# 288 empty bytes ahead of the residual stream's tile

## The chip, the cores and the metric

The kernel runs on one core of one Trainium2 chip. The metric is the device time of one execution in microseconds (us), from three runs. The profile is of one execution; its span is the time from the first to the last instruction of the program.

## The reference

A decoder trunk of two layers on a residual stream x of 512 tokens by 1024 channels, in float32:

```
for l in range(DEPTH):                                   # DEPTH = 2
    x = x + 0.5 * swiglu_ffn(x, ffn1_norm[l], ffn1_w_gate[l], ffn1_w_up[l], ffn1_w_down[l])
    h = rms_norm(x, mix_norm[l])
    p = h @ w_in[l]                                      # columns split into four head groups
    y = concat[pool_mixer, rwkv7_mixer, nsa_mixer, short_conv_mixer]
    x = x + y @ w_out[l]
    x = x + 0.5 * swiglu_ffn(x, ffn2_norm[l], ffn2_w_gate[l], ffn2_w_up[l], ffn2_w_down[l])

def swiglu_ffn(x, g, w_gate, w_up, w_down):              # D_FF = 2816
    h = rms_norm(x, g)
    return (jax.nn.silu(h @ w_gate) * (h @ w_up)) @ w_down
```

Most of the work is in the projections: gate, up and down of two FFNs in each layer, w_in and w_out.

## The kernel before

**Layout.** Activations lie transposed: channels on the 128 partitions, the 512 tokens along the row. x is one tile of 8 x 512 float32, 16,384 bytes in each partition.

**The split projection.** Every projection runs in `mm3` (lines 209 to 211). A float32 weight tile w is cut by `split` into two fp32r tiles, wh (`cut`, line 203, ScalarE) and wl, the rest (line 204, VectorE). The activations are split in the same way: hh and hl for a normed input, ah and al for the gated FFN middle, yh and yl for the mixers' output. Each slice k of 128 input channels then takes three matmuls of a stationary 128x128 weight slice by a moving 128x512 tile, wh by hh, wh by hl, wl by hh, all added up in one PSUM tile:

```
for k in range(n):
    sl = slice(k * P, (k + 1) * P)
    self.nc.tensor.matmul(ps, wh[:, sl], xh[:, k], start=(first and k == 0), stop=False)
    self.nc.tensor.matmul(ps, wh[:, sl], xl[:, k], start=False, stop=False)
    self.nc.tensor.matmul(ps, wl[:, sl], xh[:, k], start=False, stop=(last and k == n - 1))
```

**An FFN** (`ffn`) has two halves of 11 blocks. A block has 8 slices for gate and 8 for up, so 48 matmuls into the PSUM tiles d and r, and gives one slice of ah and al. Behind each half stands a down projection: 8 output tiles with 11 slices each, so 33 matmuls for each, into d and n in turn. FFN1 reads hh and hl from the pool `hp`. FFN2 reads another pair of tiles of the same names and shapes, from the pool `h2`, which `mix` opens behind x. The output projection (w_out, in `mix`) reads yh and yl, which lie in `hp` again.

**Weights** come by DMA through two tiles w (1024 KB for gate and up of one block, 704 KB for a down tile) and through two tiles each of wh and wl.

**The mixers** (`mixers`) work between w_in and w_out, with many small matmuls. For them x is closed (`self.xes.close()`) and its place is given to the pool `mp`; x goes to DRAM (xd) before and comes back after. Inside them, L670 is the last step of the compressed keys' scores, L573 the product of attention weights and values.

**Order.** The tile framework orders each engine's instructions by a simulated timeline and places the pools one behind the other in each partition. The places that matter here, in bytes from the start of the partition's row, are these (x is opened anew by `open_x` after each set of mixers, at the same place):

| tile | pool | begins at | remainder of 512 |
|---|---|---|---|
| hh (and yh) | hp | 29,920 | 224 |
| hl (and yl) | hp | 46,304 | 224 |
| w, two | wst | 62,688 and 70,880 | 224 |
| wh, two | wsp | 79,072 and 83,168 | 224 |
| wl, two | wsp | 87,264 and 91,360 | 224 |
| small tiles | sm | 95,456 | |
| t, five of 2,080 bytes | tp | 98,592 | |
| sq | xp | 108,992 | 448 |
| x | xp | 111,040 | 448 |
| ah, al in FFN1 | ap | 127,424 and 149,952 | 448 |
| hh, hl for FFN2 | h2 | 127,424 and 143,808 | 448 |
| ah, al in FFN2 | ap | 160,192 and 182,720 | 448 |
| the mixers' tiles | mp | 108,992 up to 228,992 | various |

The slices of hh, hl, ah and al are 2,048 bytes long and those of wh and wl 512, so all slices of a tile begin at the tile's remainder.

Of the kernel before, what the change touches and what calls it, by code (L numbers as in the profile page):

```python
# [10 lines left out]
F32 = mybir.dt.float32  # L11
# [7 lines left out]
P = 128  # L19
# [79 lines left out]
class Net:  # L99
# [266 lines left out]
    def open_x(self):  # L366
        self.xes = ExitStack()
        xp = self.xes.enter_context(self.tc.tile_pool(name=self.nm("xp"), bufs=1))
        self.sq = xp.tile([P, S], F32, tag="sq", name=self.nm("sq"))
        self.x = xp.tile([P, NCH, S], F32, tag="x", name=self.nm("x"))  # L370

    def mt(self, name, shape, dt=F32, bufs=None):
# [777 lines left out]
```

## Time and profile before

| what | us |
|---|---|
| median of 3 runs | 2114.76 |
| lowest, highest run | 2101.97, 2114.92 |
| the profiled execution, first to last instruction | 2112.0 |
| TensorE busy in it | 2086.9 |
| VectorE, ScalarE, GpSimd busy | 998.0, 683.4, 258.0 |

The profiled execution's own time is its span, 2112.0; what lies around the span is not in the trace, and the median of the runs is 2.76 above it. The busy time of TensorE is the time in which at least one matmul was under way; matmuls overlap each other, so one can last longer than the distance to the next. In the names, PE is TensorE and PEld its weight load, DVE VectorE, ACT ScalarE, POOL GpSimd. `d<-hh,wh` is a matmul into the PSUM tile d of the moving tile hh by the weight tile wh; L209 is line 209 of the kernel.

### The profile page before, as it was taken

Reading aid. Unit: us, or ns where it says so; the run is one execution under the profiler, and the core shown is the slowest. Engines: PE = TensorE matmul, PEld = TensorE weight load, DVE = VectorE, ACT = ScalarE, POOL = GpSimd, SP = SyncE. Lnnn points to the kernel's source line nnn. Section 1 sums busy time; section 2 is a strip of 40 time slices with the busy share of each in tenths; the row PEclk is TensorE's granted clock in tenths of the full one; section 3 lists DMA queues with packets and bytes.
Section 4 is the critical chain, followed back from the end, with each engine's and each line's share of the span. In section 5 each row is a group of like instructions: output and inputs, shape, how many; then the busy total and the mean of one; then the engine's idle time right before and its main releaser. Section 6 shows DMA issues by size and latency. Waiting matters only on the chain.

```text
span 2112.0 us, 25358 instructions
## 1 busy us (share of the span) xinstructions
PE 2086.9 (99%) x10262; PEld 1662.1 (79%) x10262; DVE 998.0 (47%) x1792; ACT 683.4 (32%) x1101; POOL 258.0 (12%) x249
## 2 busy tenths in 40 slices
PE   8999999999999999999999999999999999999999
PEld 6888888777668888888888888887776688888887
DVE  5434434567555443433544344356674544334333
ACT  4222323332464322222332223233324643222221
POOL 1100111113001110011011001110120011100110
PEclk9999999999799999999999999999996999999999
DMA  5223224324003222322322232242240032223223
GB/s 201 89 86 107 95 88 132 110 86 116 36 2 110 98 82 83 108 100 81 109 97 87 91 103 93 92 137 84 95 119 21 1 119 81 94 83 113 94 84 91
DMA packets 60438, 195.20 MB, mean 92 GB/s; under 512 B 29344, under 2 KB 29472, under 8 KB 45600
## 3 DMA queue, kind: packets, MB, share of 16 engines
q1 hardware_dynamic: 57760, 185.18, 27.2%
q0 software_dynamic: 2560, 8.39, 1.1%
q8 instruction: 80, 1.31, 0.3%
q14 instruction: 38, 0.31, 0.0%
HBM read 183.58 MB, written 8.93 MB: 91 GB/s over the span
## 4 chain that ended last, share of the span: by engine, by line
PE 97%; DVE 2%; ACT 0%; issue 0%; DMA 0%; SPq 0%; DVEq 0%
PE d L209 15%; PE d L211 15%; PE d L210 15%; PE r L211 8%; PE r L210 8%; PE r L209 8%; PE n L210 5%; PE n L211 5%; PE n L209 5%; PE o L573 2%; PE d L544 2%; PE n L561 1%; PE r L935 1%; PE n L622 1%; PE c L826 1%; PE c L823 0%
## 5 line engine op out<-in xcount | busy, mean ns | idle before, releaser
L203 ACT CAST wh<-w 128x1024 fp32r<-128x1024 f32 (+2 forms) x360 | 343.9, 955 | 1113.8 <-issue 333.4
L204 DVE TENSOR_TENSOR wl<-w,wh 128x1024 fp32r<-128x1024 f32 (+2 forms) x360 | 400.3, 1112 | 225.7 <-ACT wh L203 218.8
L209 PE MATMUL d<-hh,wh 128*128 128x512 f32 x1008 | 399.2, 396 | 6.9 <-ACT hh L216 6.9
L210 PE MATMUL d<-hl,wh 128*128 128x512 f32 x1008 | 397.8, 395 | 2.4 <-DVE hl L217 2.4
L211 PE MATMUL d<-hh,wl 128*128 128x512 f32 x1008 | 397.1, 394 | 0.0
L210 PE MATMUL r<-hl,wh 128*128 128x512 f32 x736 | 289.1, 393 | 0.0
L211 PE MATMUL r<-hh,wl 128*128 128x512 f32 x736 | 288.8, 392 | 0.0
L209 PE MATMUL r<-hh,wh 128*128 128x512 f32 x736 | 288.7, 392 | 0.0
L270 POOL TENSOR_TENSOR al<-t,ah 128x512 fp32r<-128x512 f32 x88 | 151.9, 1726 | 1084.5 <-ACT ah L269 1084.5
L209 PEld LDWEIGHTS d<-hh,wh 128*128 128x128 f32 x1008 | 189.8, 188 | 52.3 <-ACT hh L216 6.9
L210 PEld LDWEIGHTS d<-hl,wh 128*128 128x128 f32 x1008 | 189.8, 188 | 45.9 <-DVE hl L217 4.5
L211 PEld LDWEIGHTS d<-hh,wl 128*128 128x128 f32 x1008 | 189.9, 188 | 43.6 <-issue 2.3
L264 DVE TENSOR_TENSOR t<-d,rs 128x512 f32<-128x512 f32 x88 | 60.5, 691 | 274.3 <-PE d L211 268.3
L268 DVE TENSOR_TENSOR t<-t,r 128x512 f32<-128x512 f32 x88 | 60.5, 687 | 227.8 <-PE r L211 227.6
L210 PEld LDWEIGHTS r<-hl,wh 128*128 128x128 f32 x736 | 138.2, 188 | 30.9
L209 PEld LDWEIGHTS r<-hh,wh 128*128 128x128 f32 x736 | 138.2, 188 | 30.9
L211 PEld LDWEIGHTS r<-hh,wl 128*128 128x128 f32 x736 | 138.2, 188 | 30.8
L210 PE MATMUL d<-al,wh 128*128 128x512 f32 x352 | 139.2, 396 | 0.0
L211 PE MATMUL n<-ah,wl 128*128 128x512 f32 x352 | 139.2, 396 | 0.0
L209 PE MATMUL n<-ah,wh 128*128 128x512 f32 x352 | 139.2, 396 | 0.0
L209 PE MATMUL d<-ah,wh 128*128 128x512 f32 x352 | 139.2, 395 | 0.0
L211 PE MATMUL d<-ah,wl 128*128 128x512 f32 x352 | 139.2, 395 | 0.0
(297 smaller groups left out, 2348.6 us busy)
## 6 DMA issues: line engine op xcount, KB each, us to landing
w<-in_g SPq DMA_DIRECT2D x87, 1024.0 KB, 4.9
w<-in_d SPq DMA_DIRECT2D x64, 704.0 KB, 4.1
w<-in_win SPq DMA_DIRECT2D x20, 1024.0 KB, 4.9
w<-in_wout SPq DMA_DIRECT2D x8, 1024.0 KB, 5.8
xd<-x POOLq DMA_DIRECT2D x16, 256.0 KB, 4.1
x<-xd POOLq DMA_DIRECT2D x16, 256.0 KB, 5.6
x<-in_x SPq DMA_DIRECT2D x8, 256.0 KB, 5.4
s<-in_cmpk SPq DMA_DIRECT2D x8, 256.0 KB, 3.5
```

The lines of the kernel that those rows point to most:

```text
L203: self.nc.scalar.copy(hi, w)
L204: self.nc.vector.tensor_sub(lo, w, hi.bitcast(F32))
L209: self.nc.tensor.matmul(ps, wh[:, sl], xh[:, k], start=(first and k == 0), stop=False)
L210: self.nc.tensor.matmul(ps, wh[:, sl], xl[:, k], start=False, stop=False)
L211: self.nc.tensor.matmul(ps, wl[:, sl], xh[:, k], start=False, stop=(last and k == n - 1))
L264: nc.vector.tensor_mul(t, pg, self.rs)
L268: nc.vector.tensor_mul(th, th, pu)
L270: nc.gpsimd.tensor_sub(al, th, ah.bitcast(F32))
L544: nc.tensor.matmul(pq[:, :w], Q[j][hs, i * P:(i + 1) * P], kt[hs, :w], start=True, stop=True)
L561: nc.tensor.transpose(ptr[:, b * P:(b + 1) * P], sc[:, b * P:(b + 1) * P], self.ident)
L573: nc.tensor.matmul(po["o"][64 * hp:64 * hp + 64], VT[:, b, br * 64:br * 64 + 64], pT[:, b * P:(b + 1) * P], start=False, stop=(br == 1 and ...
L622: nc.tensor.matmul(ph[0:31, 0:P], blk[:, l], w1[:, (l % 4) * P:(l % 4 + 1) * P], start=(l == 0), stop=(l == 15))
```

## The change

`open_x` takes one more tile between sq and x, of 72 float32 values, 288 bytes in each partition. Nothing writes or reads it. x, and the pools `ap` and `h2` that stand behind it, then begin 288 bytes further on: x at 111,328, ah and al of FFN1 at 127,712 and 150,240, FFN2's hh and hl at 127,712 and 144,096, its ah and al at 160,480 and 183,008. The remainder of 512 is 224 for each of them. hp, the weights, the small tiles, sq and the mixers' tiles stay where they are.

```
         self.sq = xp.tile([P, S], F32, tag="sq", name=self.nm("sq"))
+        xp.tile([P, 72], F32, tag="gap", name=self.nm("gap"))
         self.x = xp.tile([P, NCH, S], F32, tag="x", name=self.nm("x"))
```

## Rows read from the trace of the kernel before

**Rows 1.** The page, busy time of each engine, share of the span, instructions.
```profile
PE 2086.9 (99%) x10262; PEld 1662.1 (79%) x10262; DVE 998.0 (47%) x1792; ACT 683.4 (32%) x1101; POOL 258.0 (12%) x249
```

**Rows 2.** The page, the chain that ended last, by engine and by line.
```profile
PE 97%; DVE 2%; ACT 0%; issue 0%; DMA 0%; SPq 0%; DVEq 0%
PE d L209 15%; PE d L211 15%; PE d L210 15%; PE r L211 8%; PE r L210 8%; PE r L209 8%; PE n L210 5%; PE n L211 5%; PE n L209 5%; PE o L573 2%; PE d L544 2%; PE n L561 1%; PE r L935 1%; PE n L622 1%; PE c L826 1%; PE c L823 0%
```

**Rows 3.** Windows by stage; the first line names the columns.
```profile
core 0: us, PE busy (x) PEld busy (x) DVE busy (x) ACT busy (x) POOL busy (x), PEclk, DMA share, GB/s
134.50:195.50 61.00, 61.00 (x263) 49.11 (x262) 23.38 (x31) 13.00 (x17) 1.28 (x1) 1.00 0.33 106
197.50:315.00 117.50, 117.50 (x520) 97.27 (x519) 47.51 (x54) 33.26 (x42) 18.10 (x10) 1.00 0.28 93
656.50:686.50 30.00, 30.00 (x134) 24.84 (x133) 15.74 (x20) 11.52 (x17) 5.54 (x3) 1.00 0.31 105
708.50:1057.50 349.00, 349.00 (x1497) 281.05 (x1496) 146.86 (x178) 100.53 (x131) 41.66 (x25) 1.00 0.29 94
...
1360.50:1422.00 61.50, 61.50 (x265) 49.54 (x264) 30.54 (x41) 21.97 (x32) 9.13 (x11) 1.00 0.43 135
1757.50:2106.50 349.00, 349.00 (x1497) 280.96 (x1496) 138.73 (x167) 90.87 (x116) 37.66 (x22) 1.00 0.29 93
```

**Rows 4.** Timeline of TensorE in FFN1: start, duration; first and last of 28.
```profile
219.80 0.39 PE L210 MATMUL d<-hl,wh 128*128 128x512 f32 x1
...
225.92 0.39 PE L210 MATMUL r<-hl,wh 128*128 128x512 f32 x1
```

**Rows 5.** Timeline of TensorE in FFN2: start, duration; first and last of 25.
```profile
749.79 0.40 PE L209 MATMUL r<-hh,wh 128*128 128x512 f32 x1
...
755.39 0.40 PE L209 MATMUL d<-hh,wh 128*128 128x512 f32 x1
```

**Rows 6.** Timeline of TensorE from the output projection into FFN2.
```profile
685.75 0.39 PE L210 MATMUL n<-yl,wh 128*128 128x512 f32 x1
685.97 0.39 PE L211 MATMUL n<-yh,wl 128*128 128x512 f32 x1
686.20 0.39 PE L209 MATMUL n<-yh,wh 128*128 128x512 f32 x1
686.43 0.39 PE L210 MATMUL n<-yl,wh 128*128 128x512 f32 x1
686.65 0.39 PE L211 MATMUL n<-yh,wl 128*128 128x512 f32 x1
686.88 0.40 PE L209 MATMUL d<-hh,wh 128*128 128x512 f32 x1
687.11 0.40 PE L210 MATMUL d<-hl,wh 128*128 128x512 f32 x1
687.35 0.40 PE L211 MATMUL d<-hh,wl 128*128 128x512 f32 x1
```

**Rows 7.** The page, groups of instructions: busy, mean ns | idle before, releaser.
```profile
L209 PE MATMUL d<-hh,wh 128*128 128x512 f32 x1008 | 399.2, 396 | 6.9 <-ACT hh L216 6.9
L210 PE MATMUL d<-hl,wh 128*128 128x512 f32 x1008 | 397.8, 395 | 2.4 <-DVE hl L217 2.4
...
L210 PE MATMUL d<-al,wh 128*128 128x512 f32 x352 | 139.2, 396 | 0.0
```

**Rows 8.** The page, DMA issues: KB each, us from issue to landing.
```profile
w<-in_g SPq DMA_DIRECT2D x87, 1024.0 KB, 4.9
w<-in_d SPq DMA_DIRECT2D x64, 704.0 KB, 4.1
```

**Rows 9.** Windows of TensorE, compression to end of attention, each layer: PEclk third.
```profile
532.00:641.30 109.30, 106.63 (x947) 0.86 0.03 11
1576.70:1690.60 113.90, 111.22 (x948) 0.82 0.03 11
```

**Rows 10.** The chain that ended last in order of time: start, us.
```profile
531.93 1.73 PE n L670 x16
...
641.27 1.51 PE o L573 x16
...
1576.68 1.73 PE n L670 x16
...
1690.53 1.51 PE o L573 x16
```

More of the change, by code (lines that the diff above doesn't have):

```diff
@@ L369, in open_x @@
         self.sq = xp.tile([P, S], F32, tag="sq", name=self.nm("sq"))
+        xp.tile([P, 72], F32, tag="gap", name=self.nm("gap"))
         self.x = xp.tile([P, NCH, S], F32, tag="x", name=self.nm("x"))
```

## Prediction

> **What bounds the kernel now.** I read the page's busy times first: TensorE is busy for 2086.9 of 2112.0 us [rows 1], and the chain that ended last is 97% TensorE, nearly all of it three source lines, L209 to L211, the three matmuls of the split projection [rows 2]. So the end is set by how fast these matmuls follow each other. Their busy time does not tell that: a record lasts 0.39 or 0.40 us, but the next one starts before it has ended. What counts is the **pitch**, the distance from start to start, and the change can act on nothing else, as it adds no instruction.
>
> So the second reading is the pitch by stage. In a stretch without idle time, the number of records is (width + one record) / pitch, since a record that juts into the stretch is counted too. The first layer's FFN1, second half, gate and up: (117.5 + 0.39) / 520 = 0.2267 us. FFN2 of either layer: (349.0 + 0.40) / 1497 = 0.2334 us. The down projection of FFN1: (61.0 + 0.40) / 263 = 0.2335 us. The output projection: (30.0 + 0.39) / 134 = 0.2268 us [rows 3]. The timeline gives the same two numbers more finely: 27 starts from 219.80 to 225.92, so 226.7 ns, and 24 starts from 749.79 to 755.39, so 233.3 ns [rows 4, 5].
>
> Now the third reading: what do the slow stretches share? The clock is granted in full in all of them [rows 3], the tile shapes are equal, the weights come through the same two pairs of buffers. FFN1 and FFN2 run the very same code. The one thing that splits them is where the moving tile lies: hh, hl, yh and yl in the pool hp at remainder 224 are fast; ah, al and FFN2's hh, hl, all behind x at remainder 448, are slow. The switch falls on one instruction: between 685.75 and 686.65 us the output projection steps by 0.22 to 0.23 with records of 0.39, and from 686.88 on, the first matmul that reads FFN2's hh, records are 0.40 long and steps 0.23 to 0.24 [rows 6]. In rows 4 and 5 the pitch is also the same over all eight weight slices of a tile, which lie 512 bytes apart, and when the second weight buffer takes over. So if the pitch hangs on how moving and weight tile lie to each other, it repeats every 512 bytes.
>
> **The change part by part.** It is one edit with one direct effect: x and all that is stacked on it move up by 288 bytes, and 448 + 288 = 736 = 512 + 224. Behind it ah, al, and FFN2's hh and hl begin at remainder 224, as the weights and the tiles of hp do.
>
> - Matmuls that move to the fast offset. Down projections: six groups (three terms, two accumulators) of 352, of which one is shown, 2112 matmuls [rows 7]. FFN2 gate and up: 22 blocks x 2 x 8 slices x 3 = 1056 in each layer, 2112 in both. Sum 4224.
> - Gain of each: 233.3 - 226.7 = 6.67 ns [rows 4, 5]. 4224 x 6.67 = **28.2 us**. All of it lies on the path, because TensorE has no idle time in these stretches [rows 3]. I take the full 6.67 since the other end of the comparison is the same code on tiles at the very remainder that the moved ones get. The bounds for this term are 0 (the remainder is not the cause) and 28.2.
> - What is late next: the supply of weights. At the fast pitch a gate/up block takes 48 x 226.7 = 10.9 us and its 1024 KB land in 4.9; a down block takes 33 x 226.7 = 7.5 us and its 704 KB land in 4.1 [rows 8], with two buffers. FFN1 already feeds the fast pitch with the same loads. In the busiest down stretch VectorE works 30.54 of 61.5 us and ScalarE 21.97 [rows 3]; 3% less room does not matter. If that cover were gone in the down stages alone, their half of the gain, 14.1 us, would be lost.
> - What else moves: x changes its remainder for VectorE, ScalarE, GpSimd and the DMAs. No row shows what that does to such an instruction. The nearest rows are TensorE's waits on the feed that reads x, 6.9 and 2.4 us in the whole run [rows 7]; if those instructions changed by a tenth either way, it would be 1 us. I take zero and keep +-1. The tiles of the mixers do not move at all, since they are opened when x is closed; the norm's sq lies ahead of the gap. FFN2's al, the highest tile behind x, ends at byte 205,248, below the mixers' top at 228,992, so nothing is pushed out.
>
> The profiled span falls from 2112.0 to 2083.8. The median of the runs shown is 2.76 us above that span; I carry this over: 2114.76 - 28.2 = **2086.6 us**, 1.3% less. About 1%, 21 us here, is what a measurement of this kernel can tell from no change, so the forecast lies just beyond.
>
> The unchanged part has a spread that matters more than this sum's error. In the stage from the compression to the end of attention the granted clock averages 0.86 in the first layer and 0.82 in the second [rows 9], that is 30.6 and 41.0 us at 1.2 instead of 2.4 GHz, where the work before was small matmuls. The same instructions took 641.27 - 531.93 = 109.34 us in the first layer and 1690.53 - 1576.68 = 113.85 in the second [rows 10]: 4.5 us for 10.4 us more at the low level, 0.43 us each. So both stretches cost about 31 us, the first alone 13 us, which is just how far the fastest of the three runs lies below the other two (2101.97 against 2114.8). A median can land 13 us lower in this way, or some us higher.
>
> **The rivals.**
> *It is the place, not the remainder.* All fast moving tiles end below byte 62,688 and all slow ones begin at 127,424 or above, so a border anywhere between, or a period longer than 512 bytes in the address of the moving tile itself, would leave the same rows. Shifting by 288 bytes would change nothing: 2114.8 us. Against it: within the upper part the pitch is the same at 127,424 and at the top of al, 78 KB higher. Nothing in the rows excludes it. The Trainium skill speaks for no effect as well: "SBUF — State Buffer", section "Who interferes with whom", says of the ports that TensorE never waits on anyone, and "TensorE: Matmul & The Clock Gate", section "Step-by-step: what each phase is for", that loading the next weights takes no read bandwidth from the running matmul; by these the offset to the weight tile could not matter and the time would be 2114.8. The trace does not bear out that matmuls of one shape all run alike: 226.7 against 233.3 ns with the weight load overlapped in both. Chance 0.13.
>
> *Half of it.* Something other than the offset holds the down projections (two arrays of 11 slices, weights of 6 and 5 slices) at 233.3. Against it: FFN2's gate and up have the same pitch with other tiles, loads and block lengths. Price 2112 x 6.67 = 14.1 us, so 2100.7. Chance 0.06.
>
> *Slower: more time at the low clock.* The mixers start 3.5 us earlier in the first layer, and if the stage from the compression on fell to 1.2 GHz for longer, at 0.43 us per us, it could eat the gain. The stage has 223 us in both layers together, 71.6 of them low now [rows 9]. From 71.6 + 28.2 / 0.43 = 137 low us on, it ends slower than before; a loss of over 1% takes 71.6 + 49.3 / 0.43 = 186; with all 223 low the time would be 2086.6 + 65 = 2152. For it: the stage has had 30.6 and 41.0 us for the same work, so it varies. Against: nothing in that stage changes, and the three runs lie within 13 us. Chance 0.03.
>
> **How the numbers follow.** Forecast 0.78, no effect 0.13, half 0.06, slower 0.03. The forecast's own range is 2072 (one low stretch less, 13 us, and a little) to 2092. The range must leave out no more than 0.2: it drops the no-effect and the slower case and reaches over the half: 2072 to 2102. Faster by over 1% (below 2093.6): the forecast's 0.78 less about a tenth, for a run with longer low stretches, 0.71. Within 1%: no effect, half, and that tenth, less a little of the no-effect case that a spell of low clock pushes out: 0.25. Slower 0.04.
>
> **What would show it.** In the changed kernel's profile: records of 0.39 us and a pitch of 226.7 ns in FFN2 and in the down projections, no step at the first matmul of FFN2, and stretches of 349.0 us that hold (349.0 + 0.39) / 0.2267, about 1541 records. FFN1's gate and up and the output projection must stay at 226.7. If the pitch behind x stays at 233.3, the first rival holds; if it falls in FFN2's gate and up alone, the second; if all pitches fall and the time does not, look at the granted clock in the attention stages. A pitch between the two levels, or the hp tiles turning slow, would mean that I have the wrong relation altogether; so would a different order of instructions in the mixers.

## The result, and the profile after

The changed kernel takes 2086.14 us in the median of four runs (2084.97 to 2087.51), the kernel before 2114.84 in the median of its four (2101.97 to 2124.65). The ratio is 0.987, with a 95% interval of 0.985 to 0.990: 1.3% faster. The forecast was 2086.6.

The profiled execution's span is 2083.2 us, against 2112.0: 28.8 less. The page's busy times of the changed kernel answer to [rows 1]:

```profile
PE 2057.5 (99%) x10262; PEld 1660.9 (80%) x10262; DVE 998.2 (48%) x1792; ACT 683.3 (33%) x1101; POOL 258.7 (12%) x249
```

TensorE has lost 29.4 us of busy time with the same 10262 matmuls; VectorE, ScalarE and GpSimd work as long as before, to within 1 us. So it is not that something waits less: TensorE does the same work in less time. The windows by stage of the changed kernel answer to [rows 3] (columns: stretch, width, busy time of each engine with its instructions, granted clock, DMA share, GB/s):

```profile
134.50:193.50 59.00, 59.00 (x262) 48.90 (x261) 23.42 (x31) 13.08 (x17) 1.30 (x1) 1.00 0.33 109
194.50:313.00 118.50, 118.50 (x524) 98.21 (x523) 48.75 (x56) 33.82 (x43) 18.11 (x10) 1.00 0.27 93
652.50:682.00 29.50, 29.50 (x132) 24.45 (x131) 15.47 (x20) 11.24 (x16) 5.55 (x3) 1.00 0.31 107
704.00:1042.50 338.50, 338.50 (x1495) 280.32 (x1494) 147.01 (x178) 100.20 (x131) 41.88 (x25) 1.00 0.29 97
...
1739.50:2077.50 338.00, 338.00 (x1493) 279.97 (x1492) 138.66 (x167) 90.27 (x115) 37.90 (x22) 1.00 0.29 96
```

The same arithmetic as before, (width + one record) / number, gives one pitch for all five: 59.39 / 262 = 226.7 ns in FFN1's down projection, 118.89 / 524 = 226.9 in its gate and up, 29.89 / 132 = 226.4 in the output projection, 338.89 / 1495 = 226.7 and 338.39 / 1493 = 226.7 in the two FFN2. The counts are whole records, so the last digit is no more than that. TensorE is still busy without a gap in each of them. And the step at the first matmul of FFN2 [rows 6] is gone; this is the same place in the changed kernel's timeline (start, duration):

```profile
682.14 0.39 PE L210 MATMUL n<-yl,wh 128*128 128x512 f32 x1
682.37 0.39 PE L211 MATMUL n<-yh,wl 128*128 128x512 f32 x1
682.59 0.39 PE L209 MATMUL d<-hh,wh 128*128 128x512 f32 x1
682.82 0.39 PE L210 MATMUL d<-hl,wh 128*128 128x512 f32 x1
683.05 0.39 PE L211 MATMUL d<-hh,wl 128*128 128x512 f32 x1
```

The records stay at 0.39 and the steps at 0.22 to 0.23 on both sides of 682.59. The attention stages, of which nothing was to change, answer to [rows 9] and [rows 10]; first the windows of TensorE, then the chain in order of time (lines have moved down by one below the edit):

```profile
528.40:637.00 108.60, 105.62 (x948) 0.87 0.03 11
1558.40:1672.20 113.80, 111.13 (x948) 0.82 0.03 11
```

```profile
528.40 1.73 PE n L671 x16
...
636.99 1.51 PE o L574 x16
...
1558.38 1.73 PE n L671 x16
...
1672.15 1.51 PE o L574 x16
```

From mark to mark it is 108.59 and 113.77 us, against 109.34 and 113.85: 0.8 us less in both together. So 28.0 of the 28.8 us lie outside the attention stages, where the projections are.

### The profile page after: what moved, and what is told of

Read it like the earlier page. It is cut to its first block, busy times and chain, and to the rows that moved or that the text cites. A ratio compares the mean times of both kernels' runs of the same rounds, so it can differ in the third digit from the quotient of the medians.

```text
span 2083.2 us, 25358 instructions
## 1 busy us (share of the span) xinstructions
PE 2057.5 (99%) x10262; PEld 1660.9 (80%) x10262; DVE 998.2 (48%) x1792; ACT 683.3 (33%) x1101; POOL 258.7 (12%) x249
## 4 chain that ended last, share of the span: by engine, by line
PE 97%; DVE 2%; ACT 0%; issue 0%; DMA 0%; SPq 0%; DVEq 0%
PE d L209 15%; PE d L211 15%; PE d L210 15%; PE r L211 8%; PE r L209 8%; PE r L210 8%; PE n L211 5%; PE n L209 5%; PE n L210 5%; PE o L574 2%; PE d L545 2%; PE n L562 1%; PE r L936 1%; PE n L623 1%; PE c L827 1%; PE c L824 0%
## 5 line engine op out<-in xcount | busy, mean ns | idle before, releaser
L210 PE MATMUL d<-hl,wh 128*128 128x512 f32 x1008 | 395.7, 393 | 2.7 <-DVE hl L217 2.7
L211 PE MATMUL d<-hh,wl 128*128 128x512 f32 x1008 | 394.9, 392 | 0.0
L210 PE MATMUL r<-hl,wh 128*128 128x512 f32 x736 | 287.0, 390 | 0.0
L211 PE MATMUL r<-hh,wl 128*128 128x512 f32 x736 | 286.8, 390 | 0.0
L210 PEld LDWEIGHTS d<-hl,wh 128*128 128x128 f32 x1008 | 189.8, 188 | 44.2 <-DVE hl L217 5.3
L211 PEld LDWEIGHTS d<-hh,wl 128*128 128x128 f32 x1008 | 189.8, 188 | 41.3 <-issue 2.3
L211 PEld LDWEIGHTS r<-hh,wl 128*128 128x128 f32 x736 | 138.2, 188 | 28.6
L210 PEld LDWEIGHTS r<-hl,wh 128*128 128x128 f32 x736 | 138.2, 188 | 28.5
L211 PE MATMUL n<-ah,wl 128*128 128x512 f32 x352 | 137.1, 389 | 0.0
L210 PE MATMUL d<-al,wh 128*128 128x512 f32 x352 | 137.0, 389 | 0.0
L211 PE MATMUL d<-ah,wl 128*128 128x512 f32 x352 | 137.0, 389 | 0.0
```

## The experiments

In all of them the arithmetic and the instructions' order on each engine are those of the kernel before; only places in the partition's row differ. The **offset** is the moving tile's remainder less the weight tile's, modulo 512; the change takes the tiles behind x from 224 to 0. The pitch of a stage is the mean of its steps from start to start in the timeline, without the few steps over 262 ns; past the first 20 us, most of these are the first step behind a group of small matmuls.

**Weights moved instead of tiles (swap).** 224 empty bytes behind hp put the weights at remainder 448, and 288 ahead of x put x back at 448 (w, the small tiles, t, sq and the mixers' tiles, which stand behind hp too, move by the same 224):

```
     h = net.htiles(net.hp)
+    net.hp.tile([P, 56], F32, tag="hgap", name=net.nm("hgap"))
...
         self.sq = xp.tile([P, S], F32, tag="sq", name=self.nm("sq"))
+        xp.tile([P, 72], F32, tag="gap", name=self.nm("gap"))
```

> The weight tiles are moved to remainder 448 by 224 empty bytes behind hp; everything behind x is put back at 448, hp stays at 224. Theory 1 (the relation of moving to weight tile, modulo 512, decides): the pitches change places, FFN2 and the down projections run at 226.7 ns, FFN1's gate and up, the input and the output projection (3504 matmuls) at 233.3; time 2114.8 - 28.2 + 23.4 = 2110. Theory 2 (the moving tile's own remainder decides, 224 fast and 448 slow, wherever the weights lie): every pitch as before the change, 2114.8.

The pitches changed places. Windows of this kernel: FFN1's down projection, FFN1's gate and up, FFN2 of the first layer:

```profile
137.50:196.50 59.00, 59.00 (x262) 48.86 (x261) 23.54 (x31) 13.36 (x17) 1.30 (x1) 1.00 0.34 109
197.50:319.50 122.00, 122.00 (x525) 98.01 (x524) 48.99 (x56) 34.19 (x43) 18.12 (x10) 1.00 0.27 90
...
715.00:1052.50 337.50, 337.50 (x1490) 279.57 (x1489) 146.26 (x178) 100.15 (x130) 41.89 (x25) 1.00 0.30 97
```

59.39 / 262 = 226.7 ns where ah and al are read, 122.40 / 525 = 233.1 where hp's hh and hl are, 337.89 / 1490 = 226.8 in FFN2. The tiles of hp have not moved by a byte and have become slow; those behind x have kept their remainder 448 and have become fast. So neither the place of the moving tile nor its own remainder decides, but its relation to the weights. That refutes theory 2, and with it the rival of the place.

The time was to be 2110. The profiled execution took 2108.74, but the median of the five is 2093.85 (ratio to the kernel before 0.991, interval 0.989 to 0.992). The mean granted clock tells why: it was 0.982 in the first and 0.990 to 0.991 in the four others, which took 2093.5 to 2095.6. This is the spread that the prediction read from [rows 9] and [rows 10]; more on it below.

**Which offsets are fast (scan1, scan2).** A gap ahead of each pool behind x, of another size in each stage, and a gap between hp and the weights (64 bytes in scan1, 32 in scan2):

```
+GAPS = [320, 352, 32, 416, 448, 32]          # scan1; scan2: [32, 64, 32, 128, 160, 32]
...
+    def gap(self, pool):
+        n = next(self.gaps)
+        if n:
+            pool.tile([P, n // 4], F32, tag="gap", name=self.nm("gap"))
...
+            self.gap(ap)                     # first in each FFN's pool ap
+        self.gap(hp)                         # first in FFN2's pool h2
...
+    net.hp.tile([P, 16], F32, tag="hgap", name=net.nm("hgap"))   # scan2: 8
```

> Seven offsets of the moving tile against the weight tile (modulo 512) in one kernel: 448 in hp (weights at remainder 288), and behind x 32, 64, 96 in the first layer (FFN1 down, FFN2 gate and up, FFN2 down), 128, 160, 192 in the second. Theory 1 with a step (only equal remainders are fast): 233.3 ns in every projection, 2114.8 + 23.4 = 2138. Theory 1 with a slope: pitches between 226.7 and 233.3 that grow with the distance. Theory 2: hp stays at 226.7, as its tiles have not moved, and the others depend on their own remainders 320 to 480.

> Seven more offsets: 480 in hp (weights at remainder 256), behind x 256, 288, 320 in the first layer and 352, 384, 416 in the second. Theory 1 with a step: 233.3 ns everywhere, 2138. With a slope: the farthest, 256, is the slowest, over 233.3 if 224 already costs 6.7. Theory 2: hp at 226.7, the others by their own remainders 0 to 160. An offset with a pitch below 226.7 would be a better place than the change's.

One run each: 2125.07 us at a clock of 0.986 and 2130.48 at 0.982, so neither kernel is worth having, and both are under the 2138 that a step would give. The pitches, with 0 and 224 from the changed kernel and the one before:

| offset | ns | offset | ns |
|---|---|---|---|
| 0 | 226.7 | 256 | 226.8 |
| 32 | 233.3 | 288 | 233.3 |
| 64 | 228.9 | 320 | 228.9 |
| 96 | 233.3 | 352 | 233.4 |
| 128 | 232.4 | 384 | 232.4 |
| 160 | 234.3 | 416 | 234.3 |
| 192 | 233.3 | 448 (hp) | 233.3 |
| 224 | 233.3 | 480 (hp) | 233.3 |

For example, FFN1's down projection at 32 in scan1 and at 256 in scan2, in windows of those two kernels:

```profile
137.50:198.50 61.00, 61.00 (x263) 49.01 (x262) 23.53 (x31) 13.26 (x17) 1.29 (x1) 1.00 0.33 106
```

```profile
138.00:197.00 59.00, 59.00 (x262) 48.87 (x261) 23.24 (x31) 12.94 (x17) 1.31 (x1) 1.00 0.34 109
```

61.40 / 263 = 233.4 and 59.39 / 262 = 226.7. Three things follow. hp's tiles, again unmoved, are slow in both kernels, so theory 2 falls a second time. The right column repeats the left: **the relation repeats every 256 bytes**, not 512. And it is neither a step nor a slope: 64 costs 2.2 ns, 160 costs 7.6, and 256, which a slope would make the slowest, costs nothing. No offset among them is better than 0.

**A gap of 32 bytes (gap32).** If 256 bytes are the period, x need only go from 448 to 480:

```
         self.sq = xp.tile([P, S], F32, tag="sq", name=self.nm("sq"))
+        xp.tile([P, 8], F32, tag="gap", name=self.nm("gap"))
```

> The gap is 32 bytes in place of 288, so all that lies behind x begins 256 bytes off the weights' remainder (480 against 224). If the relation repeats every 256 bytes, as the scans of offsets say, FFN2 and the down projections run at 226.7 ns and the time is that of the change, 2086. If 512 is the period, they stay slow and the time is that of the kernel before, 2114.

Measured: 2086.21 us (2085.00 to 2087.97), ratio to the kernel before 0.988 (0.984 to 0.991), the same span as the changed kernel's, 2083.2. FFN2 of the first layer holds as many matmuls in the same stretch as in the changed kernel's row, 1495:

```profile
704.00:1042.50 338.50, 338.50 (x1495) 280.24 (x1495) 146.94 (x178) 100.17 (x130) 41.90 (x25) 1.00 0.29 97
```

So the change's whole gain comes with a ninth of its gap, though the remainders of 512 are then 480 and 224: equal remainders of 512 are enough, but more than is needed.

**Less than 32 bytes (sub32).** The changed kernel, with the tiles behind x made 128 elements wider and read 1, 2, 3, 4, 5 or 7 elements in:

```
+OFFS = [1, 2, 3, 4, 5, 7]
...
+                ah = ap.tile([P, NFH * S + 128], F32R, tag="ah", name=self.nm("ah"))
+                ah = ah[:, o:o + NFH * S].rearrange("p (c s) -> p c s", s=S)
```

(al, hh and hl likewise.)

> The changed kernel, with the moving tiles behind x read 4, 8, 12 bytes (first layer: FFN1 down, FFN2 gate and up, FFN2 down) and 16, 20, 28 bytes (second layer) beyond equal remainders. If only whole units of 32 bytes count, some of these stay at 226.7 ns; if the exact start counts, all are slower, like 32 with 233.3. A pitch below 226.7 would be a better place.

One run, 2118.98 us. The pitches: 4 bytes 238.0 ns, 8 bytes 232.8 to 233.2, 12 bytes 228.9, 16 bytes 231.7, 20 bytes 239.9, 28 bytes 228.7. So the exact start counts, and 20 bytes are the worst offset of all that were tried, 13.2 ns a matmul. The row is the second layer's FFN2, gate and up of its second half, at 20 bytes:

```profile
1926.00:2051.00 125.00, 125.00 (x523) 100.51 (x522) 48.45 (x56) 33.64 (x43) 18.01 (x10) 1.00 0.26 88
```

125.40 / 523 = 239.8 ns, by whole records.

**Only wl moved (wl_apart).** The changed kernel, with 224 bytes between wh and wl (and the gap ahead of x cut to 64, so that all else stays at remainder 224):

```
+        self.wsp.tile([P, 56], F32, tag="wgap", name=self.nm("wgap"), bufs=1)
         lo = self.wsp.tile([P, 1024], F32R, tag="wl", name=self.nm("wl"))
...
+        xp.tile([P, 16], F32, tag="gap", name=self.nm("gap"))
```

> The changed kernel, but with wl alone at remainder 448; wh, hp and all behind x are at 224. Theory 1a (the weight load that runs beside the matmul counts, that of the next matmul): the step that starts at the second matmul of a slice, wh by hl, beside which wl is loaded, is 233.3 ns, the two others 226.7. Theory 1b (the weights with which the matmul works count): the step that starts at the third, wl by hh, is the slow one. Either way a third of 7728 matmuls is slower by 6.7 ns: 2086 + 17 = 2103. Theory 2: 226.7 throughout, 2086.

One run, 2113.30 us at 0.986, so about 10 more than either theory said. The mean pitch is 231.1 ns in all stages, 4.4 over the best, where one slow step in three would make 2.2. By steps it is 228.3 from wh by hh, 229.2 from wh by hl, 235.8 from wl by hh. First FFN1's down projection in this kernel's windows, 59.39 / 257 = 231.1 ns, then its timeline (the edit moves the three matmuls to L210, L211 and L212):

```profile
137.00:196.00 59.00, 59.00 (x257) 47.93 (x256) 22.87 (x31) 12.59 (x16) 1.30 (x1) 1.00 0.33 109
```

```profile
240.14 0.39 PE L210 MATMUL r<-hh,wh 128*128 128x512 f32 x1
240.37 0.39 PE L211 MATMUL r<-hl,wh 128*128 128x512 f32 x1
240.60 0.40 PE L212 MATMUL r<-hh,wl 128*128 128x512 f32 x1
240.84 0.39 PE L210 MATMUL r<-hh,wh 128*128 128x512 f32 x1
241.06 0.39 PE L211 MATMUL r<-hl,wh 128*128 128x512 f32 x1
241.29 0.40 PE L212 MATMUL r<-hh,wl 128*128 128x512 f32 x1
```

That the moving tiles have stayed at their place shows once more that the weights' place counts. But both forms of the theory fall as they were put: one weight tile of two costs two thirds of the whole price, 13.3 ns for three matmuls where all off by 224 cost 20. Theory 1b comes nearer: 9.1 of the 13.3 fall on the step that starts at wl by hh. The small tiles, t and sq have moved by 224 bytes in this kernel, as they had in the swap. They are not the cause of the long step: it comes back at every third matmul, the one by wl, while VectorE, ScalarE and GpSimd, which work on those tiles, have 31, 16 and 1 instructions to 257 matmuls in the row above.

**Moving tiles apart (pairs).** Different offsets for the two moving tiles of a stage, by gaps ahead of each (ah and al, hh and hl), as in the scans.

```
+GAPS = [288, 224, 0, 288, 0, 256, 288, 128, 416, 384, 64, 96]
...
+                if half == 0:
+                    self.gap(ap, "gap2")     # between ah and al
...
+        for t in ("hh", "hl"):
+            self.gap(hp, "gap" + t)
+            nh.append(hp.tile([P, NCH, S], F32R, tag=t, name=self.nm(t)))
```

> Behind x the two moving tiles of a projection get different offsets against the weights. First layer: down of FFN1 (ah 0, al 224), FFN2 gate and up (hh 224, hl 0), FFN2 down (0, 256); second layer: (0, 128), (128, 0), (64, 160). If each matmul pays for its own moving tile alone, al off by 224 costs 6.7 ns in one step of three (mean pitch 228.9), hh off by 224 costs it in two (231.1), (0, 256) costs nothing, and the slow step is that of the tile that is off. If neighbours count too, as two slow steps of three with wl off suggest, one tile that is off spoils two steps (231.1 in both cases).

One run, 2096.77 us. Mean pitch by (offset of hh or ah, offset of hl or al): (0, 224) 231.1, (224, 0) 233.3, (0, 256) 226.7, (0, 128) and (128, 0) both 228.9, (64, 160) 230.4. The rows are FFN1's down projection at (0, 224) and FFN2's gate and up at (224, 0):

```profile
135.00:194.00 59.00, 59.00 (x257) 47.96 (x257) 22.91 (x31) 12.71 (x17) 1.29 (x1) 1.00 0.34 109
867.00:989.00 122.00, 122.00 (x525) 98.15 (x524) 48.60 (x56) 33.88 (x43) 18.11 (x10) 1.00 0.27 90
```

59.40 / 257 = 231.1 ns and 122.40 / 525 = 233.1. In the stage with (0, 224) the steps are 227.8, 233.3 and 232.2: two are slow, that of al and the next. In (0, 128) only al's own step is, 234.0 against 226.7 and 226.0, and in (128, 0) the two of hh are, 232.4 and 228.4 against 225.9. So a matmul does not pay for its own tile alone, the theory with neighbours holds at (0, 224), and it does not hold at (224, 0), where all three are slow. (0, 256) costs nothing, as the period of 256 says.

## Why the prediction was right

**The pitch is the bound.** It held: 28.2 us were worked out from 4224 matmuls at 6.67 ns, and the span fell by 28.8, 28.0 of it outside the attention stages. All stages behind x went from 233.3 to 226.7, those of hp stayed, and nothing else took the time back.

**The cause is the offset to the weights.** The rows of before allowed three readings: place, own remainder, relation. The prediction chose on the equal pitch of the same code at another address and held the place for a rival at 0.13. The swap settles it: unmoved tiles became slow and tiles at an unmoved remainder fast when the weights were shifted. What was shifted with them (small tiles, t, sq) is set aside by two other kernels: in pairs nothing but what lies behind x has moved, and the pitch changes all the same, and in wl_apart the long step is that of the matmul by wl. The Trainium skill's rules spoke for no effect ("SBUF — State Buffer", section "Who interferes with whom": TensorE never waits on anyone; "TensorE: Matmul & The Clock Gate", section "Step-by-step: what each phase is for": a weight load takes no read bandwidth from the running matmul). The trace does not agree with no effect: the same instructions in the same order run at 226.7 ns where moving and weight tile have equal remainders and at 233.3 where these differ by 224 bytes. That the read of the moving tile and the read of the weights collide is my reading of it and not shown; no run had matmuls without weight loads beside them.

**The period.** The inference that it repeats every 512 bytes (from the weight slices, which lie 512 apart) was right but loose: it is 256. It made no difference to the time.

**What was late next.** Nothing: TensorE is busy for the whole width of every window above, with VectorE and ScalarE no longer at work than before. The half-gain rival (down projections held back) is out, as they run at 226.7 too.

**x itself.** I took zero and kept 1 us. TensorE's waits on the feed are 6.9 and 2.7 us in the changed kernel's groups, against 6.9 and 2.4:

```profile
L209 PE MATMUL d<-hh,wh 128*128 128x512 f32 x1008 | 396.9, 394 | 6.9 <-ACT hh L216 6.9
L210 PE MATMUL d<-hl,wh 128*128 128x512 f32 x1008 | 395.7, 393 | 2.7 <-DVE hl L217 2.7
```

**The spread by the clock.** The prediction priced it at 0.43 us for each us at 1.2 GHz. The kernel before, run again beside gap32, took 2101.88 us at a mean clock of 0.990, 2114.38 at 0.983 and 2124.78 at 0.977. That is about 42, 72 and 98 us at the low level (twice the missing share of the time): 22.9 us for 56, 0.41 each. So the 13 us that the fastest of the first runs lay below the others fit the clock, as the prediction read it; the clocks of those first runs are not on record, but 2101.97 is within 0.1 of the later run at 0.990. The changed kernel's four runs all had 0.983 or 0.984, the level of the profiled execution of before. With the clock of the swap's later runs it would have come out some 15 lower, at 2071, just below the range; that it agreed to half a microsecond is luck.

**The slower rival** did not come: 108.59 and 113.77 us between the marks, 0.87 and 0.82 of the clock.

## What to carry to other kernels

When TensorE is busy without a gap, compare the distance from start to start of equal matmuls between stages: 3% that no wait and no idle time shows was visible there, and its cause was found by asking what the slow ones share. Where moving and weight tiles are fp32r and a weight load stands beside each matmul, as here, try to place them so that their starts differ by a multiple of 256 bytes; 32 empty bytes were worth 28 us in this kernel, and 224 put in behind hp took 3504 matmuls from 226.7 to 233.3 ns. Check the mean granted clock of each run before a difference of about 1% is put down to an edit: runs of the kernel before lay 1.1% apart, 2101.88 us at 0.990 and 2124.78 at 0.977.

## What the runs showed of the hardware

The pitch of these 128x128 by 128x512 fp32r matmuls goes by the distance between moving and weight tile, and it repeats after 256 bytes at all eight distances that were tried 256 apart: 226.7 ns at 0, 228.7 to 239.9 ns at the others, without an order in the distance (20 bytes 239.9, 28 bytes 228.7, 64 bytes 228.9, 160 bytes 234.3). The three matmuls of a slice affect one another: one tile alone off by 224 bytes costs 4.4 ns a matmul in the mean where it is wl or al and 6.7 where it is hh; wh alone was not tried. How the two reads meet stays open; that would take a kernel that streams with no weight load beside it, which was not tried, nor were offsets between 32 and 256 bytes that are no multiple of 32, or other shapes and types.
